# Small native fp32 matmuls set between the dense blocks of a two-layer decoder trunk

## The chip, the core and the metric

The kernel runs on one core of one Trainium2 chip. The time is that of one execution on the device, in microseconds. Beside the time of whole executions there is a profile of one of them, which records every instruction of the engines: TensorE (PE for matmuls, PEld for its weight loads), VectorE (DVE), ScalarE (ACT), GpSimdE (POOL) and SyncE (SP), which issues most of the DMA transfers.

## The reference

The reference computes two decoder layers on a sequence of 256 tokens of width 1024, all in float32. Cut to what matters here:

```python
def reference(x, ...):
    for layer in range(2):
        h = rms_norm(x, norm[layer])
        if layer % 2 == 0:   # RG-LRU recurrence and stick-breaking attention side by side
            x = x + ab_mixer(h, ...)      # projection 1024 -> 2560, output projection 1024 -> 1024
        else:                # S5 state-space layer and MoBA softmax attention side by side
            x = x + cd_mixer(h, ...)      # projection 1024 -> 2048, output projection 1024 -> 1024
        h = rms_norm(x, ffn_norm[layer])
        x = x + (silu(h @ w_gate) * (h @ w_up)) @ w_down      # hidden width 2816
    return rms_norm(x, final_norm)
```

Nearly all arithmetic is in the projections and in the two feed-forward layers, matrix products with 256 columns of activations.

## The kernel before

Activations lie transposed: 128 features on the partitions, the 256 tokens in the free dimension. The weights come from memory as 186 pieces of 128 x 1024 float32 (512 KB), in the order of use. Each piece holds eight blocks of 128 x 128.

To keep float32 accuracy at the faster float32r matmul, each weight piece and each activation is split into a high part and a remainder. ScalarE copies the piece into `hi` (line 109), VectorE subtracts to get `lo` (line 112). A weight block then takes three matmuls: high by high, high weight by low activation, low weight by high activation. I call these three a triple. `dense` (line 152, matmuls at line 160) runs a list of weight blocks into one accumulation group in PSUM; `dense2` (matmuls at line 169) runs two groups in an interleaved order; `proj_v` (line 368) uses matmuls of 512 columns.

The program for TensorE and SyncE runs in the order in which it is written; the other engines' order is planned. `next_block` hands out the weight blocks, issues the load of the piece six ahead and the split of the piece three ahead.

Between the dense blocks stand other matmuls, mostly native fp32, that is, matmuls whose operands are float32 and not float32r. Each shows in the trace as two MATMUL records. They are: the means and broadcasts of the norms (`rstd_a`, line 241, one column; `rstd_b`, line 260, 128 columns), the recurrence's gates (412, 413), the attention scores (448, 449), suffix sums (463, float32r), products with the values (473, 475), Toeplitz matrices of the state-space layer (`toep`, 780), transposes (771, 934), its state inputs (`v_mm`, 852, 64 columns), its outputs (903), and the second attention (914, 915, 941, 942).

The state inputs of line 852 are a special case. `v_mm` puts 16 of them as closures into a list, `fill`, and `pop_fill` takes one off after every third dense matmul, so that during two of the odd layer's projection blocks a native matmul of 64 columns stands after every triple.

A feed-forward layer (`ffn`) has eleven pairs and two down passes. A pair computes two gate and two up blocks of the hidden layer: four dense blocks of eight triples. The order is pairs 0 to 6, the down product of the first 12 hidden blocks, pairs 7 to 10, the down product of the last 10 hidden blocks. In pair 0 the norm's matmuls stand between the up blocks. In the first feed-forward, hooks behind pairs 7 and 9 and behind a late down output add the Toeplitz matmuls and transposes that prepare the state-space layer.

All of these other matmuls, and the second outputs of `dense2`, take their PSUM tiles from a pool of four buffers, `axt()`; dense blocks take theirs from another pool of four.

Of the kernel before, what the change touches and what calls it, by code (L numbers as in the profile page):

```python
# [36 lines left out]
TURNS = [(i, k) for k in range(8) for i in range(2)]  # L37
LAST_K = [(i, k) for i in range(2) for k in range(7)] + [(0, 7), (1, 7)]
LAST_C = [(i, c) for i in range(2) for c in range(8)] + [(i, c) for i in range(2) for c in (8, 9)]
FFN_ORDER = (*(("pair", j) for j in range(7)), ("down", 0, 12, False),  # L40
             *(("pair", j) for j in range(7, 11)), ("down", 12, 22, True))

# [7 lines left out]
def trunk_kernel(  # L50
# [93 lines left out]
    fill = []  # L144
    beat = [0]

    def pop_fill():
        beat[0] += 1
        if fill and beat[0] % PACE == 0:
            fill.pop(0)()  # L150

    def dense(ps, ah, al, ks, at=None):
        n = len(ks)
        at = at or (lambda k: (ah[:, k, :], al[:, k, :]))
        for j, k in enumerate(ks):
            wh, wl = next_block()
            h_, l_ = at(k)
            terms = ((wh, h_), (wh, l_), (wl, h_))
            for i, (w, a) in enumerate(terms):
                PE.matmul(ps, lhsT=w, rhs=a, start=(j == 0 and i == 0), stop=(j == n - 1 and i == 2))  # L160
                pop_fill()

    def dense2(pss, order, at):
        for n, (i, k) in enumerate(order):
# [70 lines left out]
            PE.matmul(wps[:, 0:T], lhsT=warm[:, 0:128], rhs=warm, start=True, stop=True)  # L235

    def rstd_a(last=False):
        ps = axt()
        for j in range(2):
            js = slice(j * 128, (j + 1) * 128)  # L240
            PE.matmul(ps[:, j:j + 1], lhsT=acc_t[0][:, js], rhs=mean[:, 0:1], start=True, stop=not last)
            if last:
                if j == 0:
                    idle()
                PE.matmul(ps[:, j:j + 1], lhsT=sq[:, 7, js], rhs=mean[:, 0:1], start=False, stop=True)
        if last:
            idle()
        y = rp.tile([128, 2], F32, tag="rs", name=nm("rs"))
        t = rp.tile([128, 2], F32, tag="rt", name=nm("rt"))
        S.activation(out=t, in_=ps[:, 0:2], func=AF.Sqrt, bias=junk[:, 0:1])  # L250
        V.reciprocal(y, t)
        V.scalar_tensor_tensor(out=y, in0=ps[:, 0:2], scalar=EPS / 4, in1=y, op0=ALU.add, op1=ALU.mult)
        V.tensor_add(y, y, t)
        last_v[0] = V.reciprocal(y, y)
        return y

    def rstd_b(y, copy=True):
        ps = axt()
        for j in range(2):
            PE.matmul(ps[:, j * 128:(j + 1) * 128], lhsT=y[:, j:j + 1].to_broadcast([128, 128]),  # L260
                      rhs=ident, start=True, stop=True)
        if not copy:
            return ps[:, 0:T]
        r = rp.tile([128, T], F32, tag="rstd", name=nm("rstd"))
        S.activation(out=r, in_=ps[:, 0:T], func=AF.Copy)
        return r
# [6 lines left out]
    def ffn(g_next, post, R, half=False):  # L273
        es = ExitStack()
        if half:
            half_line("f", es)
        hp = es.enter_context(tc.tile_pool(name=nm("hp"), bufs=HBUFS))
        tp = es.enter_context(tc.tile_pool(name=nm("tp"), bufs=2))
        r = [None]
        ht = {}  # L280

        def pair(j):
            first = j == 0
            pg = mmt()
            if first:
                pg2 = axt()[:, 0:T]
                dense2((pg[:, 0, :], pg2), LAST_K, at_x)
            else:
                dense(pg[:, 0, :], xh, xl, ALL)
                dense(pg[:, 1, :], xh, xl, ALL)  # L290
            pu = mmt()
            dense(pu[:, 0, :], xh, xl, ALL)
            if first:
                y = rstd_a()
                dense(pu[:, 1, :], xh, xl, ALL)
                r[0] = rstd_b(y)
            t = tp.tile([128, 2, T], F32, tag="t", name=nm("t"))
            if first:
                V.tensor_mul(t[:, 0, :], pg[:, 0, :], r[0])
                V.tensor_mul(t[:, 1, :], pg2, r[0])  # L300
            else:
                V.tensor_mul(t, pg, bc(r[0], 2))  # L302
            S.activation(out=t, in_=t, func=AF.Silu)  # L303
            R.tensor_mul(t, t, bc(r[0], 2))  # L304
            if not first:
                dense(pu[:, 1, :], xh, xl, ALL)
            h = tp.tile([128, 2, T], F32, tag="h", name=nm("h"))
            V.tensor_mul(h, pu, t)  # L308
            hh = hp.tile([128, 2, T], F32R, tag="hh", name=nm("hh"))
            hl = hp.tile([128, 2, T], F32R, tag="hl", name=nm("hl"))  # L310
            S.activation(out=hh, in_=h, func=AF.Copy)  # L311
            V.tensor_sub(hl, h, hh)
            ht[2 * j], ht[2 * j + 1] = ((hh[:, c, :], hl[:, c, :]) for c in range(2))
            post(j)

        def down(lo_, hi_, last):
            for k in range(8):
                if last and k < 2:
                    if k == 0:
                        pds = [mmt()[:, 0, :] for _ in range(2)]  # L320
                        dense2(pds, LAST_C, lambda i: ht[lo_ + i])
                    pd = pds[k]
                else:
                    pd = mmt()[:, 0, :]
                    dense(pd, None, None, list(range(lo_, hi_)), lambda i: ht[i])
                V.tensor_add(x[:, k, :], x[:, k, :], pd)  # L326
                if last:
                    x_ready(k, 1, g_next)
                    if k == 5:
                        preload_sqrt(sq[:, k, 0:1])  # L330
                    post(11 + k)

        for op, *a in FFN_ORDER:
            if op == "pair":
                pair(*a)
            else:
                down(*a)
        es.close()
# [37 lines left out]
    def layer_ab():  # L376
# [31 lines left out]
                                       in1=xc[:, i, :], op0=ALU.mult, op1=ALU.add)  # L408

        def gate_mm(i):  # L410
            ps = axt([128, 2, T])
            PE.matmul(ps[:, 0, :], lhsT=gw[:, i, :], rhs=xc[:, i, :], start=True, stop=True)
            PE.matmul(ps[:, 1, :], lhsT=gw[:, 4 + i, :], rhs=xc[:, i, :], start=True, stop=True)
            S.activation(out=tr[:, i, :], in_=ps[:, 0, :], func=AF.Sigmoid, bias=vec[:, V_BA + i:V_BA + i + 1])
            act["gate"] = S.activation(out=ti[:, i, :], in_=ps[:, 1, :], func=AF.Sigmoid,
                                       bias=vec[:, V_BX + i:V_BX + i + 1])
# [24 lines left out]
                    V.tensor_sub(yl[:, cs, :], xc[:, cs, :], yh[:, cs, :])  # L441

        def scores(h):
            ps = axt()
            p0 = 64 * (h % 2)
            q_ = qk[p0:p0 + 64, h // 2, 0, :]
            k_ = qk[p0:p0 + 64, h // 2, 1, :]
            PE.matmul(ps[:, 0:T], lhsT=k_[:, 0:128], rhs=q_, start=True, stop=True)
            PE.matmul(ps[:, T:NM], lhsT=k_[:, 128:T], rhs=q_[:, 128:T], start=True, stop=True)
            v3 = lambda a: a.rearrange("p (a b) -> p a b", a=3)  # L450
            V.scalar_tensor_tensor(out=z[:, :, h, :], in0=v3(ps[:, 0:NM]), scalar=0.125, in1=v3(msk[:, 0, :]),
                                   op0=ALU.mult, op1=ALU.add)

        def suffix(c):
            hs = slice(4 * c, 4 * c + 4)
            sph, spl = sph_[c], spl_[c]
            for p in (2, 1, 0):
                ps = axt([128, 4, 128])
                terms = [(0, p)] + ([(1, 2)] if p == 1 else [])
                n = 0  # L460
                for m, q in terms:
                    for a in (sph, spl):
                        PE.matmul(ps, lhsT=tr_r[:, m, :], rhs=a[:, q], start=(n == 0), stop=(n == 2 * len(terms) - 1))
                        n += 1
                V.tensor_sub(z[:, p, hs, :], z[:, p, hs, :], ps)
                S.activation(out=e[:, p, hs, :], in_=z[:, p, hs, :], func=AF.Exp)

        def av(j):
            ps = axt()
            for s in range(2):  # L470
                h = 2 * j + s
# [154 lines left out]
    def s5_prep(es):  # L626
# [137 lines left out]
            G.tensor_add(zi, zi, a)  # L764

        def tp(half):
            for src, dst in ((0, s5["wr"]), (1, s5["wi"])):
                for c in range(0, 8, 4):
                    ps = axt([128, 4, 128])
# [2 lines left out]
                    S.activation(out=dst[:, 8 * half + c:8 * half + c + 4, :], in_=ps, func=AF.Copy)  # L772

        def toep(q):
            ps = axt()
            for c in range(4):
                p = 4 * q + c
# [37 lines left out]
    def layer_cd():  # L815
# [41 lines left out]
            return vr, vi  # L857

        def flush():
            while fill:  # L860
                fill.pop(0)()

# [31 lines left out]
                lambda: V.memset(zi[:, :, 63:64], 0.0)))  # L894

        def y_mm(ps, q):
            for c in range(4):
                p = 4 * q + c
                w_ = lambda a: a[:, p, 1:5, :].rearrange("p a b -> p (a b)")
# [36 lines left out]
            return s_  # L936

        def moba_av(h, pt):
            po = axt()
            hs = slice(128 * h, 128 * h + 128)  # L940
            PE.matmul(po[:, 0:T], lhsT=vt[:, 0, hs], rhs=pt[:, 0:T], start=True, stop=False)
# [313 lines left out]
```

## Time and profile before

| | |
|---|---|
| median of 3 runs | 608.91 us (607.36 to 609.07) |
| the profiled execution: its own time | 608.91 us |
| the profiled execution: span of its instructions | 607.1 us |
| TensorE busy | 591.0 us, 97% of the span, 4840 matmuls |
| VectorE, ScalarE, GpSimdE busy | 438.4, 346.2 and 208.3 us |
| read from memory | 100.93 MB, 168 GB/s over the span |

The profile names each instruction by its line in the kernel, its engine and its tiles, `out<-in`. A line that groups instructions gives their count, their busy time together and the mean duration of one, and the idle time of the engine just before them with what ended it. Matmuls overlap, so their durations add up to more than the time they take; the distance from the start of one to the start of the next tells the rate. In the view in order of time, the first column is the start in microseconds from the span's beginning and the second the duration.

### The profile page before, as it was taken

Reading aid. Unit: us, or ns where it says so; the run is one execution under the profiler, and the core shown is the slowest. Engines: PE = TensorE matmul, PEld = TensorE weight load, DVE = VectorE, ACT = ScalarE, POOL = GpSimd, SP = SyncE. Lnnn points to the kernel's source line nnn. Section 1 sums busy time; section 2 is a strip of 40 time slices with the busy share of each in tenths; the row PEclk is TensorE's granted clock in tenths of the full one; section 3 lists DMA queues with packets and bytes.
Section 4 is the critical chain, followed back from the end, with each engine's and each line's share of the span. In section 5 each row is a group of like instructions: output and inputs, shape, how many; then the busy total and the mean of one; then the engine's idle time right before and its main releaser. Section 6 shows DMA issues by size and latency. Waiting matters only on the chain.

```text
span 607.1 us, 11926 instructions
## 1 busy us (share of the span) xinstructions
PE 591.0 (97%) x4840; PEld 576.0 (95%) x4840; DVE 438.4 (72%) x636; ACT 346.2 (57%) x480; POOL 208.3 (34%) x203
## 2 busy tenths in 40 slices
PE   8899999999999999999999999999999999999995
PEld 7799889999899999999999998899999999999994
DVE  5798998896999976637857992797756655556632
ACT  6769996942443535465656268766545434344452
POOL 0810001539999999159810000022121110021131
PEclk9999999999999999999999999999999999999998
DMA  8746345753465774536544422455555555655501
GB/s 314 257 155 194 108 161 183 243 153 128 144 198 181 240 226 156 174 105 201 181 162 128 143 91 70 167 177 189 177 194 177 189 190 181 201 174 186 196 1 70
DMA packets 29319, 102.76 MB, mean 169 GB/s; under 512 B 3520, under 2 KB 3536, under 8 KB 29264
## 3 DMA queue, kind: packets, MB, share of 16 engines
q1 hardware_dynamic: 28080, 99.36, 50.0%
q10 hardware_dynamic: 864, 1.57, 0.7%
q0 software_dynamic: 320, 1.06, 0.5%
q8 instruction: 38, 0.62, 0.4%
q14 instruction: 17, 0.14, 0.1%
HBM read 100.93 MB, written 1.05 MB: 168 GB/s over the span
## 4 chain that ended last, share of the span: by engine, by line
PE 73%; DVE 12%; ACT 6%; POOL 3%; issue 3%; DMA 2%; SPq 0%; DVEq 0%; POOLq 0%; ACTq 0%
PE mm L160 64%; DVE lo L112 3%; PE mm L169 3%; ACT u L907 1%; ACT hi L109 1%; DMA raw<-wall 1%; DMA x<-xT 1%; PE ax L169 1%; PE ax L780 1%; POOL acc L217 1%; PE mm L903 1%; PE ax L852 1%; ACT s5tt L785 1%; POOL s5st L715 1%; PE ax L260 1%
## 5 line engine op out<-in xcount | busy, mean ns | idle before, releaser
L112 DVE TENSOR_TENSOR lo<-raw,hi 128x1024 fp32r<-128x1024 f32 x184 | 245.2, 1339 | 95.4 <-ACT hi L109 95.2
L109 ACT ACTIVATE hi<-raw 128x1024 fp32r<-128x1024 f32 (+1 forms) x188 | 195.2, 1048 | 179.7 <-PE mm L160 104.9
L160 PE MATMUL mm<-xh,hi 128*128 128x256 f32 x896 | 254.6, 284 | 0.8 <-ACT xh L943 0.7
L160 PE MATMUL mm<-xh,lo 128*128 128x256 f32 x896 | 250.5, 280 | 2.2 <-DVE lo L112 2.2
L160 PE MATMUL mm<-xl,hi 128*128 128x256 f32 x896 | 250.6, 280 | 0.2
L160 PEld LDWEIGHTS mm<-xh,lo 128*128 128x128 f32 x896 | 167.8, 187 | 3.0 <-DVE lo L112 3.0
L160 PEld LDWEIGHTS mm<-xh,hi 128*128 128x128 f32 x896 | 168.4, 188 | 1.7 <-ACT xh L943 1.2
L160 PEld LDWEIGHTS mm<-xl,hi 128*128 128x128 f32 x896 | 168.3, 188 | 0.9 <-DVE xl L944 0.8
L160 PE MATMUL mm<-hl,hi 128*128 128x256 f32 x312 | 87.3, 280 | 0.0
L160 PE MATMUL mm<-hh,hi 128*128 128x256 f32 x312 | 87.2, 280 | 0.0
L160 PE MATMUL mm<-hh,lo 128*128 128x256 f32 x312 | 87.1, 279 | 0.0
L215 POOL TENSOR_TENSOR acc<-sq 128x256 f32<-128x256 f32 x5 | 4.9, 987 | 185.0 <-ACT sq L211 185.0
L304 POOL TENSOR_TENSOR t<-t,rstd 128x512 f32<-128x512 f32 x11 | 18.9, 1722 | 132.7 <-ACT t L303 132.7
L160 PEld LDWEIGHTS mm<-hh,hi 128*128 128x128 f32 x312 | 58.6, 188 | 0.0
L160 PEld LDWEIGHTS mm<-hl,hi 128*128 128x128 f32 x312 | 58.5, 187 | 0.0
L160 PEld LDWEIGHTS mm<-hh,lo 128*128 128x128 f32 x312 | 58.4, 187 | 0.0
L217 POOL TENSOR_TENSOR acc<-acc,sq 128x256 f32<-128x256 f32 x29 | 27.6, 950 | 24.5 <-ACT sq L211 23.3
L311 ACT ACTIVATE hh<-h 128x512 fp32r<-128x512 f32 x22 | 13.7, 622 | 25.5 <-DVE h L308 25.5
L326 DVE TENSOR_TENSOR x<-x,mm 128x256 f32<-128x256 f32 x32 | 13.3, 416 | 18.8 <-PE mm L160 16.2
L303 ACT ACTIVATE t<-t 128x512 f32<-128x512 f32 x22 | 13.7, 622 | 17.0 <-DVE t L302 16.6
L227 DVE SCALAR_TENSOR_TENSOR xl<-x,vec,xh 128x256 fp32r<-128x256 f32 x32 | 21.8, 698 | 2.0 <-ACT xh L225 1.9
L308 DVE TENSOR_TENSOR h<-mm,t 128x512 f32<-128x512 f32 x22 | 15.1, 688 | 10.6 <-PE mm L160 8.4
(333 smaller groups left out, 982.1 us busy)
## 6 DMA issues: line engine op xcount, KB each, us to landing
raw<-wall SPq DMA_DIRECT2D x184, 512.0 KB, 3.5
raw<-wall ACTq DMA_DIRECT2D x4, 256.0 KB, 5.4
x<-xT SPq DMA_DIRECT2D x4, 256.0 KB, 5.1
gw<-gates SPq DMA_DIRECT2D x1, 512.0 KB, 7.2
p_b<-bst POOLq DMA_DIRECT2D x1, 512.0 KB, 4.1
p_c<-cst POOLq DMA_DIRECT2D x1, 512.0 KB, 4.8
outT<-x SPq DMA_DIRECT2D x2, 256.0 KB, 2.5
outT<-x ACTq DMA_DIRECT2D x2, 256.0 KB, 2.5
```

The lines of the kernel that those rows point to most:

```text
L109: last_hi[0] = S.activation(out=hi[p][:, cs], in_=raw[p][:, cs], func=AF.Copy)
L112: i = V.tensor_sub(lo[p][:, cs], raw[p][:, cs], hi[p][:, cs])
L160: PE.matmul(ps, lhsT=w, rhs=a, start=(j == 0 and i == 0), stop=(j == n - 1 and i == 2))
L169: PE.matmul(pss[i], lhsT=w, rhs=a, start=(j == 0 and not begun), stop=(j == 2 and i not in [o for o, _ in order[n + 1:]]))
L217: acc_t[1] = G.tensor_add(out=acc_t[0], in0=acc_t[0], in1=sq[:, k, :])
L227: i = eng.scalar_tensor_tensor(out=xl[:, k, :], in0=x[:, k, :], scalar=gk, in1=xh[:, k, :], op0=ALU.mult, op1=ALU.subtract)
L260: PE.matmul(ps[:, j * 128:(j + 1) * 128], lhsT=y[:, j:j + 1].to_broadcast([128, 128]), rhs=ident, start=True, stop=True)
L303: S.activation(out=t, in_=t, func=AF.Silu)
L304: R.tensor_mul(t, t, bc(r[0], 2))
L308: V.tensor_mul(h, pu, t)
L311: S.activation(out=hh, in_=h, func=AF.Copy)
L326: V.tensor_add(x[:, k, :], x[:, k, :], pd)
```

## The change

A new function `steady` issues one native fp32 matmul: the 128 x 128 identity as weights, its first 64 columns as moving operand, into a fresh tile of the `axt()` pool that nothing reads. `dense` calls it after the first triple of its block, unless the list `fill` holds something, and it acts only if a flag, `shaky`, is up; then it lowers the flag. The flag is raised at the start, by every function that issues other TensorE work (listed in the diff), and at the head of the feed-forward pairs 1, 2, 3, 4, 6 and 7. `dense2` and `proj_v` never call it. Nothing that the kernel returns depends on the added matmuls.

```diff
+STEADY_AT = (1, 2, 3, 4, 6, 7)
...
+    shaky = [True]
+
+    def steady(force=False):
+        if shaky[0] or force:
+            PE.matmul(axt()[:, 0:64], lhsT=ident, rhs=ident[:, 0:64], start=True, stop=True)
+            shaky[0] = False
+
     def dense(ps, ah, al, ks, at=None):
...
                 PE.matmul(ps, lhsT=w, rhs=a, start=(j == 0 and i == 0), stop=(j == n - 1 and i == 2))
                 pop_fill()
+            if j == 0 and not fill:
+                steady()
...
         def pair(j):
             first = j == 0
+            shaky[0] = shaky[0] or j in STEADY_AT
```

The line `shaky[0] = True` is added at the head of `rstd_a`, `rstd_b`, `gate_mm`, `scores`, `suffix`, `av`, `tp`, `toep`, `flush`, `y_mm` and `moba_av`.

More of the change, by code (lines that the diff above doesn't have):

```diff
@@ L237, in rstd_a @@
     def rstd_a(last=False):
+        shaky[0] = True
         ps = axt()
@@ L257, in rstd_b @@
     def rstd_b(y, copy=True):
+        shaky[0] = True
         ps = axt()
@@ L410, in gate_mm @@
         def gate_mm(i):
+            shaky[0] = True
             ps = axt([128, 2, T])
@@ L443, in scores @@
         def scores(h):
+            shaky[0] = True
             ps = axt()
@@ L454, in suffix @@
         def suffix(c):
+            shaky[0] = True
             hs = slice(4 * c, 4 * c + 4)
@@ L468, in av @@
         def av(j):
+            shaky[0] = True
             ps = axt()
@@ L766, in tp @@
         def tp(half):
+            shaky[0] = True
             for src, dst in ((0, s5["wr"]), (1, s5["wi"])):
@@ L774, in toep @@
         def toep(q):
+            shaky[0] = True
             ps = axt()
@@ L859, in flush @@
         def flush():
+            shaky[0] = True
             while fill:
@@ L896, in y_mm @@
         def y_mm(ps, q):
+            shaky[0] = True
             for c in range(4):
@@ L938, in moba_av @@
         def moba_av(h, pt):
+            shaky[0] = True
             po = axt()
```

## The prediction, made before the result was known

> **What bounds the kernel now.** I read the page first, then the busy time by stretch, then single instructions of TensorE in order of time. Of the page, the engines and one of the largest matmul groups:
>
> ```profile
> PE 591.0 (97%) x4840; PEld 576.0 (95%) x4840; DVE 438.4 (72%) x636; ACT 346.2 (57%) x480; POOL 208.3 (34%) x203
> ...
> L160 PE MATMUL mm<-xl,hi 128*128 128x256 f32 x896 | 250.6, 280 | 0.2
> ```
>
> TensorE is the bound nearly everywhere, with matmuls of 256 columns. A duration of 280 ns is not their price, since they overlap: what counts is the time from one start to the next, which I call the pitch. Busy time by stretch (first row: the columns; PEclk is the granted clock as a share of full):
>
> ```profile
> core 0: us, PE busy (x) PEld busy (x) DVE busy (x) ACT busy (x) POOL busy (x), PEclk, DMA share, GB/s
> 154.00:178.00 24.00, 23.37 (x195) 23.15 (x196) 24.00 (x18) 11.08 (x14) 23.61 (x13) 1.00 0.56 178
> 178.00:222.00 44.00, 44.00 (x376) 44.00 (x375) 40.75 (x34) 19.68 (x21) 43.69 (x25) 1.00 0.69 220
> 382.00:418.00 36.00, 35.94 (x305) 35.94 (x306) 32.23 (x46) 25.38 (x41) 6.75 (x7) 1.00 0.51 165
> 421.50:568.50 147.00, 147.00 (x1251) 147.00 (x1250) 88.11 (x92) 67.30 (x75) 18.95 (x11) 1.00 0.58 188
> 28.00:118.00 90.00, 89.53 (x680) 83.45 (x680) 81.57 (x129) 76.20 (x103) 14.02 (x25) 1.00 0.53 174
> ```
>
> Only from 154 to 178 is another engine full: VectorE, 24.00 of 24, while TensorE misses 0.63. In the second feed-forward VectorE has 59 of 147 us free.
>
> The dense matmuls have **two pitches**. The first is that of the second feed-forward, from the rows of line 160 between 421.4 and 568.4 (count, then first and last start):
>
> ```profile
> L160 PE MATMUL mm<-xh,hi x320: 279/279/365, 421.5 to 568.2; 128*128 128x256 f32 x160
> ...
> L160 PE MATMUL mm<-hh,hi x96: 279/279/279, 489.4 to 523.0; 128*128 128x256 f32 x96
> ```
>
> These 416 matmuls begin a triple each, so 415 triples, 1,245 pitches, lie between 421.5 and 568.2: 146.7 / 1,245 = 117.8 ns. I call this pace S. The second pitch stands right behind the state-space layer's native fp32 matmuls of 64 columns (line 852), which this kernel already drops between dense triples. In order of time, start and duration:
>
> ```profile
> 326.18 0.28 PE L160 MATMUL mm<-xh,lo 128*128 128x256 f32 x1
> 326.30 0.33 PE L852 MATMUL ax<-ush,s5wr 128*128 128x64 f32 x2
> 326.44 0.36 PE L160 MATMUL mm<-xh,hi 128*128 128x256 f32 x1
> 326.64 0.28 PE L160 MATMUL mm<-xl,hi 128*128 128x256 f32 x1
> 326.75 0.28 PE L160 MATMUL mm<-xh,lo 128*128 128x256 f32 x1
> ...
> 344.00 0.36 PE L160 MATMUL mm<-xh,hi 128*128 128x256 f32 x1
> 344.20 0.28 PE L160 MATMUL mm<-xl,hi 128*128 128x256 f32 x1
> 344.32 0.28 PE L160 MATMUL mm<-xh,lo 128*128 128x256 f32 x1
> ...
> 349.42 0.28 PE L160 MATMUL mm<-xh,lo 128*128 128x256 f32 x1
> ```
>
> From 344.20 to 349.42 lie 46 pitches without a break, across two accumulation groups: 5.22 / 46 = 113.4 ns. This is pace F. It is not the clock (1.00 in every stretch) and not the operands, the same tiles as at pace S before 326. It is a state into which the stream falls, and it stays: F for those 46, S for all of the 147 us. The native matmuls of 1 column (line 241) lead into S; one wait for weights led into F:
>
> ```profile
> 316.43 0.50 PE L241 MATMUL ax<-con,acc 128*128 128x1 f32 x4
> 316.79 0.36 PE L160 MATMUL mm<-xh,hi 128*128 128x256 f32 x1
> 316.99 0.28 PE L160 MATMUL mm<-xl,hi 128*128 128x256 f32 x1
> ...
> 317.70 0.28 PE L160 MATMUL mm<-xl,hi 128*128 128x256 f32 x1
> ```
> ```profile
> 13.52 0.38 PE L160 MATMUL mm<-xh,lo 128*128 128x256 f32 x1 [0.35 <-DVE lo L112]
> 13.74 0.28 PE L160 MATMUL mm<-xh,hi 128*128 128x256 f32 x1
> ...
> 14.31 0.28 PE L160 MATMUL mm<-xh,lo 128*128 128x256 f32 x1
> ```
>
> From 316.99 to 317.70 are 6 pitches of 118 ns; behind the wait for weights that ends at 13.52, from 13.74 to 14.31, 5 of 114.
>
> **The change part by part.** It removes nothing. It adds 33 matmuls of the form of line 852, each behind the first triple of a dense block, exactly where 852 stands. Count them by walking the program: 2 before 28 us; 11 from there to the end of the first feed-forward's pair 0; its pairs 1, 2, 3, 4, 6; then 4 there (pairs 7, 8, 10 and the last down block, the latter three behind Toeplitz matmuls and transposes); 3 in the odd layer's projection; 1 at its output; 7 in the second feed-forward (its first pair's last block, pairs 1, 2, 3, 4, 6, 7). Pair 5, and in the second feed-forward 8 to 10, get none: the flag is down.
>
> *Price.* From 326.18 to 326.64, two dense starts later, is 0.46 us; two pitches at S are 0.24. So 0.22 us each, repeated 32 times at line 852.
>
> *Worth.* 117.8 − 113.4 = 4.4 ns per pitch. So a matmul pays from 50 pitches on; a run of n dense matmuls has n − 5 behind it (three stand ahead, two starts are in the price).
>
> *Where it costs nothing.* The first two, the four of pairs 1 to 4 and the one at 378.8 stand ahead of a wait that something else ends:
>
> ```profile
> 22.14 0.60 PE L241 MATMUL ax<-con,acc 128*128 128x1 f32 x4 [0.31 <-POOL acc L217]
> ...
> 28.10 0.71 PE L260 MATMUL ax<-con,rs 128*128 128x128 f32 x4 [1.68 <-DVE rs L254]
> ...
> 154.03 0.39 PE L160 MATMUL mm<-xh,lo 128*128 128x256 f32 x1 [0.65 <-DVE lo L112]
> ...
> 381.60 0.38 PE L160 MATMUL mm<-xh,hi 128*128 128x256 f32 x1 [0.70 <-ACT xh L943]
> ```
>
> The first two disappear in 0.31 and 1.68; those of pairs 1 to 4 in the weight splits for which TensorE waits from 154 on (0.65 at 154.03, and 23.37 busy of 24 behind it); the one at 378.8 in the 0.70. Without that cover the seven would cost 1.5. What these stretches would gain from F is given back to the same wait, so pairs 1 to 5 count zero. 26 are paid: 5.7 us.
>
> *Pitches at F, if the state holds until the next foreign matmul or wait.* A pair is 4 blocks of 8 triples, 96; the first down pass 288; each half block of a projection 24. From 28 to 118 the runs between foreign matmuls are 96 (the last of the recurrent branch's projection and the first q, k pair), 24 and 24 (between the gates), 48 and 48 (between scores), 24, 36, 12, 12 (the output projection, cut by the suffix sums and the attention's products), 180 (its rest and pair 0's gate and first up block) and 24; less 5 each they give 473; 2.08 us against 11 × 0.22: **+0.34**, most of them too short to pay. Pair 6 and the down pass, 384: 379, **−1.45**; VectorE has 3.25 of the 44 us free there, TensorE wants 1.5, so it fits. Then runs of 96 (pair 7), 192 (8 and 9), 306 (10 and seven down outputs) and 102 (the last output, 30, the odd layer's two interleaved blocks, 48, and one more, 24): 676, four prices, **−2.09**. Odd projection: 24 and 51 give 65 pitches, and the third finds F there already; three prices: **+0.37**. Output after 382: before, 305 matmuls in 36 us are pace S there, behind the waits that end at 382; those waits stay, so I take S, **0**; F would give 300 pitches, −1.3. Second feed-forward: 24 gives 19, and the 1,488 matmuls from pair 1 to the end, six times interrupted, 1,458; 6.50 − 7 × 0.22: **−4.96**. Weights suffice there: at F a 512 KB piece of 24 matmuls is wanted every 2.72 us, 193 GB/s against 188 now, and VectorE is 60% busy.
>
> Sum: 3,070 pitches × 4.4 ns = 13.5, less 5.7: −7.8 us. The profiled execution took 608.91 us (span 607.1, so 1.8 lie around it); it is also the median shown. 608.9 − 7.8 = **601.1**.
>
> *What before does not show.* Each added matmul takes one of four buffers of the ax pool, whose earlier reader may be late; SyncE is not involved, but the dense matmuls queue behind it and the weight splits behind their buffers. The nearest row is that of the transposes, which take all four buffers at once (a group's busy time, mean, and idle time before it):
>
> ```profile
> L771 PE MATMUL ax<-con,p_zi 128*128 128x128 f32 x16 | 2.3, 276 | 0.4 <-ACT s5tt L785 0.4
> ```
>
> Bounds 0 and 0.4 us, at pair 10's insert behind them. I take 0: the triple ahead of it, some 0.4 us by the starts from 326.44 on, gives the first reader that time. How long F holds is not shown beyond 46 pitches; bounds 46 and a whole run. I take the run, since S, the same machine in its other state, shows no exit in 147 us and F none either.
>
> The Trainium skill ("TensorE: Matmul & The Clock Gate", Back-to-back issue gap) gives a warm gap of N/2.4 + 2.5, 109 ns at 256 columns, from width and clock alone, with no memory of what ran before. By that rule the added matmuls would be mere cost; the trace disagrees, with 113.4 and 117.8 at the same width and clock.
>
> **The rivals.** (1) *No entry*: pitch follows from width and clock, or 852 leads to F only among its own kind. Then 26 × 0.22 is lost: 608.9 + 5.7 = 614.6. For it: only one of the 32 is followed by a long run. Against: that run, and 113 ns behind each of the others. (2) *F leaks away* and ends on the other side: the state is set, but small upsets (a late weight, a new accumulation group) drop it into S within some 50 pitches. The point that decides is 50 paid pitches per insert; capped at 46 or 47, 902 pitches remain, 4.0 us against 5.7: 610.7. For it: behind native matmuls of other widths the stream ends in S, so S is the easier state to fall into. Against: no loss is seen in 46 pitches, and those cross a change of accumulation group. (3) *F does not outlive its pair*: runs capped at 91 give 1,474 pitches, 6.5 against 5.7: 608.1, no difference. Between this and the forecast lie all losses at single waits. (4) *VectorE takes over after 178*: the 1.45 is lost, 602.6; inside the range.
>
> **How the numbers follow.** Forecast with rival 4: 0.62. Partial loss, 603 to 608: 0.18, of which 0.14 below 607.1. Leak: 0.09; no entry: 0.04; a remainder that cancels: 0.07. About 0.3% (1.8 us) is what a measurement here tells from no change: faster 0.76, same 0.11, slower 0.13. The range goes down to 598.0 (F after 382, −1.3; the odd projection's 0.37 hidden in its waits; 1.5 from the median to the fastest run shown, 607.36) and up to 610.0, through the partial losses almost to the leak. The forecast's own range is 598 to 603.
>
> **What would show it.** Right: the added matmuls as a group of 66 records near 245 ns; line 160's matmuls at 276 instead of 280 ns; the second feed-forward's 1,488 dense starts some 5 us shorter in all; waits for weight splits near 154 longer. Wrong: 117.8 ns behind the inserts (rival 1), changes from 113 to 118 ns inside a run (2, 3), or new waits for a buffer of the ax pool.

## The result, and the profile after

The change makes the kernel slower. Median 615.62 us (614.72 to 616.46, 4 executions) against 608.99 us for the kernel before in the same series (607.36 to 609.79); ratio 1.0105, 95% interval 1.0087 to 1.0123. The forecast was 601.1, the range ended at 610.0. The profiled execution took 614.91 us, 6.0 more than the profiled one of before.

The page of the kernel after; then, of its groups of TensorE instructions (busy us, mean ns, idle time before), a dense one and the added one:

```profile
PE 599.1 (98%) x4906; PEld 584.1 (95%) x4906; DVE 441.3 (72%) x636; ACT 346.1 (56%) x480; POOL 207.7 (34%) x203
```
```profile
L168 PE MATMUL mm<-xl,hi 128*128 128x256 f32 x896 | 250.3, 279 | 0.2
...
L157 PE MATMUL ax<-con 128*128 128x64 f32 x66 | 10.9, 246 | 0.0
```

The 66 records are there, two for each of 33 added matmuls. But the dense ones last 279 ns on average, against 280 before, where a stretch at pace F shows 276. By stretch (columns as in the first row), with the second feed-forward in the last row, TensorE is full as before at the full clock:

```profile
core 0: us, PE busy (x) PEld busy (x) DVE busy (x) ACT busy (x) POOL busy (x), PEclk, DMA share, GB/s
154.00:178.00 24.00, 23.59 (x197) 23.18 (x196) 24.00 (x18) 10.12 (x12) 23.53 (x14) 1.00 0.48 154
178.00:222.00 44.00, 44.00 (x376) 44.00 (x375) 42.32 (x35) 21.16 (x23) 43.77 (x25) 1.00 0.69 218
426.10:573.98 147.88, 147.88 (x1259) 147.88 (x1258) 87.92 (x92) 67.41 (x75) 18.97 (x11) 1.00 0.57 187
```

Single instructions of TensorE in order of time (start, duration) show both halves of the story:

```profile
160.48 0.39 PE L168 MATMUL mm<-xh,lo 128*128 128x256 f32 x1 [0.37 <-DVE lo L113]
...
348.40 0.28 PE L168 MATMUL mm<-xl,hi 128*128 128x256 f32 x1
348.52 0.28 PE L168 MATMUL mm<-xh,lo 128*128 128x256 f32 x1
348.63 0.33 PE L157 MATMUL ax<-con 128*128 128x64 f32 x2
348.77 0.36 PE L168 MATMUL mm<-xh,hi 128*128 128x256 f32 x1
348.98 0.28 PE L168 MATMUL mm<-xl,hi 128*128 128x256 f32 x1
...
353.92 0.28 PE L168 MATMUL mm<-xl,hi 128*128 128x256 f32 x1
...
437.99 0.28 PE L168 MATMUL mm<-xh,lo 128*128 128x256 f32 x1
438.11 0.33 PE L157 MATMUL ax<-con 128*128 128x64 f32 x2
438.24 0.37 PE L168 MATMUL mm<-xh,hi 128*128 128x256 f32 x1
438.45 0.28 PE L168 MATMUL mm<-xl,hi 128*128 128x256 f32 x1
...
449.52 0.28 PE L168 MATMUL mm<-xh,lo 128*128 128x256 f32 x1
```

At 438.11 the price is the predicted one: 437.99 to 438.45 is 0.46 us instead of 0.24. Behind it, 94 pitches in the 11.07 us to 449.52: 117.8 ns, pace S. At 348.63 it is worse: this is the very stretch whose 113.4 ns the prediction had read as pace F, and behind the added matmul 42 pitches take 4.94 us, 117.6. The added matmul took the stream *out* of pace F. Of the 33, only the first, at 13.8 us and beside a wait for weights, is followed by pace F, and there the kernel before had it too.

Where the 6.0 us went: I paired the matmuls of the two traces in order and took the differences of their starts. The start at 28.54 before (28.85 after) is 0.31 later, and from there the lag grows by 0.22 to 0.23 at nearly every paid insert: 2.66 at 118.55, 2.98 at 177.98, 4.61 at 348.96, 4.66 at 421.48, 6.01 at 567.97. From 118.55 to 170.01, where four are inserted, it grows by 0.11 only. Waits there shrank; the views of waits (us, times, longest) of before and after:

```profile
PE ax L260 <- DVE rs L254: 2.4, 2, 1.7
PE mm L160 <- DVE lo L112: 2.2, 4, 0.7
```
```profile
PE ax L272 <- DVE e_t L596: 1.7, 1, 1.7
...
PE mm L168 <- DVE lo L113: 1.0, 2, 0.6
...
PE ax L789 <- ACT s5tt L804: 0.4, 1, 0.4
...
PE ax L490 <- DVE z L481: 0.3, 1, 0.3
```

### The profile page after: what moved, and what is told of

It is laid out like the page before. It is cut to its first block, busy times and chain, and to the rows that moved or that the text cites. A ratio compares the mean times of both kernels' runs of the same rounds, so it can differ in the third digit from the quotient of the medians.

```text
span 613.1 us, 12055 instructions
## 1 busy us (share of the span) xinstructions
PE 599.1 (98%) x4906; PEld 584.1 (95%) x4906; DVE 441.3 (72%) x636; ACT 346.1 (56%) x480; POOL 207.7 (34%) x203
## 4 chain that ended last, share of the span: by engine, by line
PE 83%; DVE 6%; ACT 3%; POOL 3%; DMA 2%; issue 1%; SPq 0%; DVEq 0%; POOLq 0%
PE mm L168 69%; PE mm L179 4%; PE mm L381 2%; DVE lo L113 2%; PE ax L179 1%; ACT u L928 1%; DMA x<-xT 1%; PE ax L799 1%; DMA raw<-wall 1%; POOL acc L227 1%; PE ax L871 1%; PE mm L924 1%; PE ax L157 1%; POOL p_tmp L728 1%; ACT s5tt L804 1%
## 5 line engine op out<-in xcount | busy, mean ns | idle before, releaser
L168 PE MATMUL mm<-xh,hi 128*128 128x256 f32 x896 | 257.4, 287 | 0.8 <-ACT xh L965 0.7
```

## The experiments

The rival reading at this point: the added matmul has the form of line 852, but not its operands. What the profile doesn't show is where they lie. By the addresses in the compiled program, the table `con`, whose first 128 columns are `ident`, begins 64 bytes past a multiple of 128 within each partition; the weights of line 852 in before (`s5wr`, `s5wi`) begin at a multiple of 128, and its moving operand at 64. I write w64 and w0 for the offset at which the weights begin. The traces do not hold these addresses; what the runs below show is the effect of shifts against each other.

**Operands.** In the second feed-forward of the kernel before, 46 inserts (added matmuls) of 64 columns in mixed order: weights from `con` or from the state-space tables, begun at w0 or w64 by a shift of 16 columns; moving operands at 0 or 64.

```diff
+    def probe():
+        wt, wo, mt_, mo, n = slots.pop(0)
+        PE.matmul(axt()[:, 0:n], lhsT=flat(wt)[:, wo:wo + 128], rhs=flat(mt_)[:, mo:mo + n], start=True, stop=True)
```

> The kernel before, with 46 native fp32 matmuls of 64 columns behind the first triple of the second feed-forward's dense blocks (pairs 1 to 6, the down outputs, pairs 7 and on), of eight kinds in shuffled order, five and more of each. They differ in where their operands begin in SBUF, modulo 128 bytes, and in the tensor: weights at 64 or 0, moving columns at 64 or 0, from the constants (the identity's tensor) or from the state-space tensors. The added matmul of the change has weights at 64 and moving columns at 64; line 852 of before has weights at 0 and moving columns at 64. Theory 'where the weights begin': the kinds with weights at 0 are followed by a pitch of 113.4 ns, those with weights at 64 by 117.8, whatever the tensor; with about half of the blocks at 113.4 the kernel takes 46 x 0.22 = 10 us more less some 3 us. Theory 'same tensor': only the kinds whose weights and columns come from different tensors lead to 113.4. Theory 'content' (an identity is nearly all zeros): only those with state-space weights. Theory 'company' (line 852 works only because it comes every third matmul): 117.8 behind every kind, and 10 us more.

One execution took 616.08 us. All 17 at w64 led to pace S, also out of pace F; of 29 at w0, 26 led to or kept pace F, and the three others found pace S and did not change it. I say that an insert enters where pace F follows it. Content, table and the moving operand's place made no difference. Two neighbours, both with weights and moving operand from `con`: at 428.83 with weights 16 columns in (w0), at 431.78 with the change's own weights (w64):

```profile
428.83 0.33 PE L210 MATMUL ax<-con 128*128 128x64 f32 x2
...
429.18 0.28 PE L220 MATMUL mm<-xl,hi 128*128 128x256 f32 x1
...
431.67 0.28 PE L220 MATMUL mm<-xh,lo 128*128 128x256 f32 x1
431.78 0.33 PE L210 MATMUL ax<-con 128*128 128x64 f32 x2
...
432.13 0.28 PE L220 MATMUL mm<-xl,hi 128*128 128x256 f32 x1
...
434.72 0.28 PE L220 MATMUL mm<-xh,lo 128*128 128x256 f32 x1
```

22 pitches each: 2.49 us, 113.2, and 2.59 us, 117.7.

**The change with its weights at w0.** All 33 as they were, only the weights 16 columns further in:

```diff
-            PE.matmul(axt()[:, 0:64], lhsT=ident, rhs=ident[:, 0:64], start=True, stop=True)
+            flat = con.rearrange("p a b -> p (a b)")
+            PE.matmul(axt()[:, 0:64], lhsT=flat[:, 16:144], rhs=ident[:, 0:64], start=True, stop=True)
```

> The changed kernel, with the weights of the added matmul taken 16 elements further into the constants' tensor, so that they begin at 0 modulo 128 bytes instead of 64; nothing else differs. Theory 'where the weights begin': the dense runs go to 113.4 ns and the time is that of the prediction's sum, about 601 us. Theories 'same tensor', 'content' and 'company': as the changed kernel, about 615.6 us.

607.27 us (605.27 to 609.56, 10 executions), ratio 0.9972, 0.9951 to 0.9993. The 64 bytes are worth some 8 us, 615.6 to 607.3. But not all of the gain is there. The profiled execution is the longest of the ten (609.56), with the granted clock at 0.75 from 28 to 32 us and at 0.72 from 384 to 390; in it 12 of the 33 are followed by pace F, the pair 6 stretch among them (rows of one line by tiles: count, duration min/median/max, first and last start):

```profile
L169 PE MATMUL mm<-hh,hi x96: 276/276/276, 192.9 to 225.2; 128*128 128x256 f32 x96
...
L169 PE MATMUL mm<-xl,hi x32: 276/276/276, 182.5 to 225.6; 128*128 128x256 f32 x32
```

276 ns throughout. In starts, 382 pitches at 113.3 without a loss, so F does outlive a whole run. The next insert kept it. The second feed-forward came to F only at its pair 3.

**Width and kind.** Inserts at w0 of other widths, later places, and float32r matmuls that take a dense matmul's own weights; each preceded by one at w64, 24 to 42 dense matmuls earlier, so that all start from pace S.

```diff
+        if kind == "r":
+            PE.matmul(axt()[:, 0:n], lhsT=wh, rhs=h_[:, 0:n], start=True, stop=True)
+        else:
+            o = 0 if kind == "reset" else 16
+            PE.matmul(axt()[:, 0:n], lhsT=flat()[:, o:o + 128], rhs=flat()[:, 0:n], start=True, stop=True)
```

> The kernel before, with 54 added matmuls in the second feed-forward's dense blocks: in every other block one with weights at 64 modulo 128 bytes (which was followed by 117.8 ns in all its cases so far, and serves to set that pace), in the blocks between one of nine kinds with weights at 0, three times each: native fp32 of 1, 16, 32, 128 or 256 columns behind the first triple, of 64 columns behind the second or third triple, and float32r of 64 or 128 columns with the dense block's own weights. Theory 'where the weights begin, whatever the width': 113.4 ns follows all nine kinds. Theory 'width': only 64 columns give 113.4. Theory 'phase' (the added matmul shifts the stream by its own length, and the pace behind it hangs on where in the slow pace's cycle it falls): some widths and some places give 113.4 each time, others never, and the float32r kinds, at a price below 0.12 us, can do it too.

One execution, 618.13 us. All 18 native ones of 1, 16, 32, 64 (behind the second or third triple) and 128 columns led to F; none of three with 256 columns did, nor any of six float32r ones, nor any of the 27 at w64. The price does not fall with the width; a single column (second row) and 64 columns both put the second dense start 0.46 us behind the last one ahead:

```profile
466.33 0.28 PE L228 MATMUL mm<-xh,lo 128*128 128x256 f32 x1
466.44 0.28 PE L217 MATMUL ax<-con 128*128 128x1 f32 x2
...
466.79 0.28 PE L228 MATMUL mm<-xl,hi 128*128 128x256 f32 x1
```

**Place and number.** One at w0 ahead of the first triple instead of behind it; then one behind each of the first three triples, 99 in all.

```diff
 (ahead of the first triple)
+        if not fill:
+            steady()
 (behind each of three)
+            if j < 3 and not fill:
+                steady(j)
```

> The version with weights at 0, with the added matmul ahead of the first triple of its block instead of behind it. Theory 'phase': behind a foreign matmul the stream starts at a fixed phase, so each place gives the same pace every time; if that is 113.4 everywhere, 601 us, if nowhere, 615. Theory 'where the weights begin' alone: 113.4 in most places, 601 to 605 us.

> The version with weights at 0, with one added matmul behind each of the first three triples of a block instead of the first alone: 99 in place of 33, so 14 us more to pay where nothing hides them, some 12 net of the waits. Theory 'phase': the three fall on three phases of the slow pace, so nearly every block of the program ends at 113.4 ns; with all 3,070 pitches at that pace, 601 + 12 = 613 us. If entry does not hang on the phase, the same share of blocks as with one, 607 + 12 = 619 us.

Ahead: 608.40 us, ratio 0.9989 (0.9967 to 1.0011); only 8 of 33 are followed by a run at pace F. Three: 615.49 us, ratio 1.0098 (1.0071 to 1.0124), and the third is followed by pace F at 31 of the 33 places, some 3,180 pitches in all, more than the 3,070 of the forecast. They are worth 3,180 x 4.4 = 14.0 us, against 99 x 0.22 = 21.8, part of it hidden in waits; the profiled execution lags 6.1 us behind that of before at its end. So the entry can be had by repeating, and the price then eats it wherever the run is short. In this trace and in that of the 33 at w0, nearly all inserts that started 115 ns behind their predecessor entered, those at 116 in part, and those at 117 to 122 did not, which gave the next theory.

**Five long runs only.** One, two or three at w0, or one at w64 and two triples later one at w0, at 181, 241, 270, 389 and 427 us by the times of after; these kernels are the changed one with its 33 inserts replaced. `event` counts the places of the change, `since` the triples behind one:

```diff
+PLAN = {(e, s + d): 16 for e, s in ((17, 0), (19, 0), (20, 0), (25, 6), (27, 0)) for d in (0, 1)}
...
+        o = PLAN.get((event[0], since[0]))
+        if o is not None:
+            PE.matmul(axt()[:, 0:64], lhsT=flat[:, o:o + 128], rhs=ident[:, 0:64], start=True, stop=True)
```

> One aligned matmul (weights at a multiple of 128 bytes) behind the first dense triple at only five places, those with long runs behind them: the first feed-forward's pair 6 stretch at 181 us, two blocks of the odd projection (241 and 270), the odd layer's output (from its seventh triple, about 389), the second feed-forward's first pair (427). About 470, 185, 300, 280 and 1,480 pitches can go from 117.8 to 113.3 ns, 2,715 x 4.45 = 12.1 us; price 5 x 0.22 = 1.1. Theory A (entry needs the weights' address and a start 115 or 116 ns behind the matmul before): a part of the five places enters, which part depends on the run; between 598 (all) and 610 (none), about 604. Theory B (the address alone decides): all five, 608.9 - 12.1 + 1.1 = 598.

> Two aligned matmuls, behind the first and the second triple at the same five places. Price 10 x 0.22 = 2.2. Theory A: a first one that fails leaves the next at 119 or at 115 to 116, so some places still fail; 602, between 599 and 608. Theory B: 599.

> Three aligned matmuls, behind the first three triples at the same five places. Price 15 x 0.22 = 3.3. Theory A: the third always starts 115 or 116 behind its predecessor and enters, so all five places run at 113.3 in every execution: 608.9 - 12.1 + 3.3 = 600.1, with a spread under 1 us. Theory C (each insert enters by an independent chance of about one half): seven of eight places, 601.6 with a spread of some us.

> At the same five places a matmul of the change's own form (weights 64 bytes past a multiple of 128) behind the first triple and an aligned one behind the third. Price 10 x 0.22 = 2.2. Theory A: the first leaves the next start at 115 or 116 whatever was before, the second enters always: 608.9 - 12.1 + 2.2 = 599.0, spread under 1 us. Theory C (a chance of one half for each aligned insert, none for the other): half of the places, 605. Theory B: 599.

One: 608.76 (606.45 to 611.63), ratio 0.9994 (0.9976 to 1.0012); the profiled execution missed all five (at the fourth the granted clock was down, 0.79 from 384 to 390 us). Two: 600.12 (599.78 to 602.93, 6 executions), ratio 0.9870 (0.9847 to 0.9894). Three: 601.41 (600.92 to 602.95), 0.9887 (0.9865 to 0.9909). w64 and w0: 600.48, 0.9893 (0.9848 to 0.9938), but with one execution at 608.23. That the address alone decides (theory B) is out by the first: one insert at w0 does nothing dependable. The sum of worth and price, though, is right: 599 to 602 was expected where the places enter, 600.1 to 601.4 measured.

**Which offsets.** Nine column offsets into `con`, each three times, each behind one at w64; and the pairs of w64 and w0 at four places, without the one at 389.

```diff
+            o = 0 if kind == "reset" else int(kind[1:])
...
-PLAN = {(e, s + d): o for e, s in ((17, 0), (19, 0), (20, 0), (25, 6), (27, 0)) for d, o in ((0, 0), (2, 16))}
+PLAN = {(e, s + d): o for e, s in ((17, 0), (19, 0), (20, 0), (27, 0)) for d, o in ((0, 0), (2, 16))}
```

> In the second feed-forward, 27 inserts of 64 columns whose weights begin 64, 80, 96, 112, 0, 16, 32, 48 or 0 bytes past a multiple of 128 (three times each, in mixed order; offset 0 twice under two columns), each preceded one block earlier by an insert at 64, which leaves the next start 115 or 116 ns behind its predecessor. Theory A as it stands (only a multiple of 128 enters): 113.3 behind the six at 0 and 117.8 behind the 21 others. Theory D (a window of 128 bytes is what counts, so everything under 64 enters): 113.3 behind 0, 16, 32 and 48, 117.8 behind 64 to 112. Theory E (64-byte lines, only 64 itself is bad): 113.3 behind all but 64. Time about 611 to 618, since 54 inserts are paid (12 us) and the gain lasts 23 to 35 pitches each.

> The pairs of inserts of the run before (one at 64 bytes, two triples later an aligned one) at four places: without the odd layer's output, where behind an entry at 382 us only about 60 pitches ran at 113.3 before the pace fell back. 60 x 4.45 = 0.27 gained there against 0.44 paid: 0.2 us faster than with five, 600.2, if the other four places enter; if the second feed-forward misses its entry in an execution, that one is 6.5 us longer.

None of the three theories holds. The kernel of nine offsets took 619.17 us, and each offset did the same all three times:

| bytes past a multiple of 128 | column offsets | pace behind, mean of 19 pitches |
|---|---|---|
| 0 | 16, 48 | 113.3 |
| 48, 96, 112 | 28, 8, 12 | 113.3 |
| 16, 32, 80 | 20, 24, 4 | 117.7 to 117.8 |
| 64 | 0 | 117.8 |

It is neither a multiple of 128 nor the line of 64 bytes, and the gap of 115 or 116 is no condition: entries here started 115 to 119 behind their predecessor, misses 115 to 121. The four places: 601.24 us, ratio 0.9901 (0.9867 to 0.9935), in two heaps: six executions at 599.5 to 601.3, four at 606.1 to 607.8. The distance is what the second feed-forward is worth (6.5), so I take these four to have missed it; no trace of one was taken.

**The moment.** Offsets that can enter (and 32, which did not), each behind w64 and then, four triples later, a float32r matmul of 64 or of 128 columns. And three kernels with a single insert at 112, 48 or 0 bytes (column offsets 12, 28, 48) at the four places.

```diff
+    ((0, (('reset', 64),)), (4, (('r', 64),))),
+    ((0, (('o28', 64),)),),
...
+PLAN = {(e, 0): 28 for e in (17, 19, 20, 27)}
```

> In the second feed-forward, 24 inserts at the column offsets 8, 12, 16, 24, 28, 48 (96, 112, 0, 32, 48 and 0 bytes past a multiple of 128), each preceded by the insert at 64 bytes and then, four triples later, by a float32r matmul of 64 or 128 columns, behind which starts so far stood 119 or 120 ns after their predecessor instead of 115 or 116. Theory F (the offset alone decides): 113.3 behind the twenty at 8, 12, 16, 28, 48, and 117.8 behind the four at 24. Theory P (the offset and the moment of the start together): some of the twenty stay at 117.8, those at 16 above all, whose entries so far all had a gap of 115 or 116. Time about 620, for 72 inserts at some 0.2 us are paid.

> One insert with weights at 112 bytes behind the first triple at four places (181, 241, 270, 427 us). Theory F: all four enter in every execution, 608.9 - 2,435 x 4.45 ns + 4 x 0.22 = 599.0, spread as of the kernel before, about 2 us from a dip of the granted clock. Theory P: it depends on the execution, single times from 599 to 610.

> As the run before, with weights at 48 bytes. Theory F: 599.0. Theory P: from 599 to 610.

> As the run before, with weights at 0 bytes but 48 columns into the table of constants instead of 16. Theory F: 599.0. Theory P: from 599 to 610. If the start address modulo 128 is all that counts, the same lottery as with 16 columns, where one insert at five places gave 606.5 to 611.6.

This is the clearest result. The kernel took 622.77 us. Behind the float32r matmul of 128 columns all ten at 0, 48, 96 and 112 entered; behind the one of 64 columns none of ten did; 32 never did. The same offset, 48 bytes, twice (line 208 is the float32r matmul, 211 the insert):

```profile
431.17 0.19 PE L208 MATMUL ax<-xh,hi 128*128 128x64 f32 x1
...
432.69 0.33 PE L211 MATMUL ax<-con 128*128 128x64 f32 x2
...
433.03 0.28 PE L222 MATMUL mm<-xl,hi 128*128 128x256 f32 x1
...
435.15 0.28 PE L222 MATMUL mm<-xl,hi 128*128 128x256 f32 x1
...
449.70 0.22 PE L208 MATMUL ax<-xh,hi 128*128 128x128 f32 x1
...
451.23 0.33 PE L211 MATMUL ax<-con 128*128 128x64 f32 x2
...
451.57 0.28 PE L222 MATMUL mm<-xl,hi 128*128 128x256 f32 x1
...
453.61 0.28 PE L222 MATMUL mm<-xl,hi 128*128 128x256 f32 x1
```

18 pitches each: 2.12 us, 117.8, and 2.04 us, 113.3. So the offset alone does not decide. What ran twelve or 24 dense matmuls earlier counts too; I call this the moment, and what in it counts is not shown. The single inserts agree: 606.23 (599.79 to 611.27), 604.72 (599.56 to 611.84) and 608.08 us (607.43 to 611.13), ratios 0.9902 (0.9867 to 0.9936), 0.9901 (0.9875 to 0.9926) and 0.9991 (0.9975 to 1.0007). Two of them, at 112 and 48 bytes, spread over the whole width between all entered and none.

**A prepared moment.** At the four places w64, four triples later a float32r matmul of 128 columns, four triples later w0. Beside it two at w0 in a row.

```diff
+PLAN = {(e, d): o for e in (17, 19, 20, 27) for d, o in ((0, 0), (4, -1), (8, 16))}
...
+        if o == -1:
+            PE.matmul(axt()[:, 0:128], lhsT=wh, rhs=h_[:, 0:128], start=True, stop=True)
```

> At the four places an insert at 64 bytes, four triples later a float32r matmul of 128 columns, four triples later an aligned insert. Price 0.22 + 0.11 + 0.22 = 0.55 each, 2.2 in all. Theory P1 (the preparation fixes the moment): all places enter in every execution, 608.9 - 10.8 + 2.2 = 600.3, and at most 2 us more from a dip of the granted clock. Theory P2 (the moment is not fixed by it): some executions miss the second feed-forward and lie at 606 to 609.

> Two aligned inserts behind the first two triples at the four places. Price 8 x 0.22 = 1.8. If both long places (181 and 427 us) enter in every execution: 608.9 - 10.8 + 1.8 = 599.9, up to 2 us more where the odd projection misses and 2 more from the clock. If the entry is a matter of chance there too: some executions at 606 to 609.

Prepared: 600.92 us (600.60 to 601.88, 4 executions), ratio 0.9865 (0.9844 to 0.9885). The profiled execution entered at all four places, and no time is long enough for a miss of the second feed-forward. Four executions are few, though: the kernel with w64 and w0 at the same places entered at all four in its profiled execution too, and four of its ten missed. Pairs: 601.82 us (600.40 to 603.95, 5 executions), 0.9871 (0.9848 to 0.9893); in the profiled one the place at 181 missed. Both beat both kernels by more than 1%. The prepared one in the second feed-forward (single instructions, then line 177 by tiles from 423.2 to 561.4 us):

```profile
419.77 0.33 PE L167 MATMUL ax<-con 128*128 128x64 f32 x2
...
421.41 0.22 PE L164 MATMUL ax<-xh,hi 128*128 128x128 f32 x1
...
422.93 0.33 PE L167 MATMUL ax<-con 128*128 128x64 f32 x2
```
```profile
L177 PE MATMUL mm<-xl,hi x311: 276/276/276, 423.3 to 561.3; 128*128 128x256 f32 x156
...
L177 PE MATMUL mm<-hh,hi x96: 276/276/276, 485.4 to 517.7; 128*128 128x256 f32 x96
```

Each row counts triples, 311 and 96; from the start at 423.3 to the one at 561.3 are 406 triples, 1,218 pitches, in 138.0 us: 113.3 ns, without a loss. The same pace holds for 1,459 pitches, to the end of the second feed-forward.

## Why the prediction was wrong

*The step that failed* is the first sentence of "The change part by part": 33 matmuls "of the form of line 852", which by the paragraph before lead to pace F, "not the operands, the same tiles as at pace S". The dense matmuls' operands were the same; those of the inserted matmul were not. What I called its form (native fp32, 64 columns, behind a triple) is not what sets the pace. At w64 none of 98 inserts in the four kernels that mix kinds led to F, wherever they stood; at other offsets the same form did. The row had one example, line 852 with one pair of tables, and I carried over what I could see in it. That the place of the weights is what cost the change its entries is shown by moving them 16 columns and nothing else: 615.62 became 607.27, and 12 places of 33 are followed by pace F instead of one. That even then 21 stayed out is the second half of the step: an entry depends on the moment too, and why is open.

*Rival 1*, no entry, was the outcome, with a chance of 0.04: 614.6 forecast for it, 614.91 in the profiled execution. That it is so close is partly luck, since terms that the sum did not hold cancel in part, as told below. What I held against it ("that run, and 113 ns behind each of the others") spoke only for line 852's own weights. Its second wording, that 852 leads to F only among its own kind, does not hold either: behind inserts at w64, single inserts with the weights of line 852 entered in the run on operands.

*Price.* Right: 0.22 us, seen as 0.22 to 0.23 at each step of the lag, and the same for 1 column and for 64.

*Where it costs nothing.* Right for the five at pairs 1 to 4 and at 383: of the waits for splits the one of 0.65 at 154.03 is gone and that of 0.60 at 157.72 is 0.37 (160.48 after), and the lag stands still from 378 to 418. Wrong for one of the first two: the wait that follows is 1.7 us in both kernels, so it was not shortened. Its releaser is late by as much as TensorE is; the lag at 28.5 is 0.31. Hence about 0.3 more. As much was won at an insert that I had counted as paid: the one at 117.81 stands ahead of the wait at 118.55, which is 0.82 us in before and 0.53 in after.

*Lost besides*: the 46 pitches at F before 349.42 became S, 0.2 us, which no term held, since I had counted only what inserts might give.

*Worth and lasting.* Right as far as the runs go: 4.4 to 4.5 ns, and F lasts: 1,483 pitches to the end of the second feed-forward behind the single insert at 112 bytes, 1,480 behind two at w0. Rivals 2 and 3 fall. Within a run I saw it end only where a start comes late, as at the wait for weights behind 161 in the kernel with 33 at w0, or near 396 in that with w64 and w0 at five places, where two starts lie 276 ns apart. In the prepared kernel the lag falls from -2.15 at 421.48 to -8.08 at 600.43: 5.93, and with the 0.55 of the three inserts 6.48, against 6.50 forecast for the same stretch.

*Rival 4.* VectorE does not take over after 178: in the prepared kernel it has 41.29 of 44 us, TensorE all 44, and 390 matmuls start where 376 did, a few of them the added ones:

```profile
178.00:222.00 44.00, 44.00 (x390) 44.00 (x389) 41.29 (x34) 19.85 (x23) 43.69 (x25) 1.00 0.68 225
```

*The ax pool*: right at the transposes, where TensorE waits 0.4 us as before, but not everywhere. At 91.34 it waits 0.27 us for VectorE's line 481, which reads `ax` tiles; at the same matmul in before the gap is 0.09 (89.06), and the lag grows there by 0.18. The term was put at 0, with a bound of 0.4.

*The chances.* 0.76 for faster rested on one unexamined link; range and chances were built from what might go wrong behind the entry, and the entry itself had 0.04.

The Trainium skill ("TensorE: Matmul & The Clock Gate", Back-to-back issue gap) would have had the added matmuls as mere cost, and the time came out so, though not for its reason. The gap that it gives, 109 ns at 256 columns, it calls that of an isolated matmul; for a stream it says that the weight loads set the spacing too. Of two paces it says nothing, and the traces hold both, 113.3 and 117.8 ns, at the granted clock of 1.00.

## What to carry to other kernels

A stream of equal matmuls can have two stable paces, and a foreign matmul in it may switch the one or the other on; measure the pitch behind it, over a long run, before spending it. When an operation is copied because of a side effect seen at one place, copy its operands' places too, or try one insert alone: the form in the listing isn't all that the hardware sees. A state that costs 0.22 us per insert and pays 4.4 ns per pitch belongs ahead of the few long runs, not ahead of every block, and is best set by two inserts (no time of 11 executions is long enough for a miss of the second feed-forward) or with a prepared moment (four executions).

## What the runs showed of the hardware that was not expected

- Matmuls of 256 columns in float32r at the full granted clock run at 113.3 or at 117.8 ns, each for more than 1,480 pitches on end. A native matmul of at most 128 columns between them can switch the pace, by where its weights begin in the partition (offsets 0, 48, 96, 112 bytes past a multiple of 128 can lead to 113.3; 16 and 80 did not in three tries each, 32 in seven, 64 in 98) and by the moment: 10 of 10 behind one preparation, 0 of 10 behind another, in one execution, with starts 116 to 118 and 115 to 117 ns behind the predecessor.
- That distance does not settle it: in the profiled execution of the single insert at 48 bytes a start 119 ns behind its predecessor entered at 177.72 us, and one 119 ns behind at 236.17 did not. What in the moment decides stays open, as does why those offsets; eight were tried, with one table's contents for most, and the PSUM buffer that an insert writes was not varied by itself.
- A wait can lead to 113.3 too: in the same execution, behind the wait for ScalarE that ends at 380.00 us, the dense matmuls run at 113.3 up to 396.44, with no insert there.
- A native matmul of 256 columns at w0 did not lead to F (0 of 3), one of 128 did (3 of 3), all of them 115 or 116 ns behind the predecessor.
- Executions of one kernel lie some 2 us apart for another reason as well: a dip of the granted clock, in these traces mostly behind the wait near 380 us. In the profiled execution of the kernel with two at w0 at five places the clock there is 0.76, where it is 1.00 in before and in after:

```profile
378.00:384.00 6.00, 5.10 (x25) 4.50 (x26) 3.84 (x7) 5.89 (x9) 0.00 (x0) 0.76 0.07 13
384.00:390.00 6.00, 6.00 (x51) 6.00 (x50) 4.44 (x6) 2.19 (x4) 0.00 (x0) 0.95 0.57 190
```

The lag of that execution against before grows by 2.0 us between 382 and 390. What sets off the dip is open; the median of a few executions can move by it, by up to 0.3% (2 of 600 us).
